# Fifteen rows of unread matmuls behind the last operations of a hybrid decoder step

## The chip, the cores and the metric

The kernel runs on one core of a Trainium2 chip. The metric is the device time of one execution in microseconds. A core has five engines that run their own instruction lists and wait for each other by semaphores: TensorE (PE; its weight loads are shown apart as PEld), VectorE (DVE), ScalarE (ACT), GpSimd (POOL) and SyncE (SP), which here issues most of the transfers.

## The reference

One inference step of one decoder layer, for a prompt of 256 tokens and 8 samples of one token, at a width of 2048. Cut to what matters:

```python
h = rmsnorm(x, g_pre_mix) * (1 + sc1) + sh1
z = h @ w_in                                  # split into the inputs of three branches
y_a = spatial_gating(u, layernorm(v))         # branch A
y_b = hgrn2(q, k, v)                          # branch B, with a state
y_c = gla(q, k, v)                            # branch C, with a state
merged = sum(sigmoid(z_gate[n]) * (y[n] @ w_branch[n]) for n in range(3))
x = x + gt1 * rmsnorm(merged @ w_out, g_post_mix)
h2 = rmsnorm(x, g_pre_mlp) * (1 + sc2) + sh2
y2 = square(relu(h2 @ w_mlp_up)) @ w_mlp_down
x = x + gt2 * rmsnorm(y2, g_post_mlp)
```

It returns x of the prompt and of the samples, the states of the branches, and the rows of v of the samples. All is in float32. Nothing of this is touched by the change.

## The kernel before, in words

The 256 prompt tokens and the 8 sample tokens are moved through TensorE together: 264 moving columns against weight tiles of 128 x 128. A float32 product is made from three products of a shorter float32 type, fp32r: each operand is split into a high and a low part (`split`, line 115: ScalarE writes the high part by a copy, VectorE the low part by a subtraction), and TensorE adds high x high, high x low and low x high in one accumulator. `granule` (lines 681 to 683) does this for nearly all of the work, 4600 times each line. Weights come from HBM in pieces of 512 KB, a few pieces ahead of use, and are split into tiles `whi` and `wlo` of [128, 2, 256]; a weight operand of a matmul is 128 columns of such a tile, in order.

The moving operands do not lie in token order. `by_two` and `apart` store the even tokens of a row in its first half and the odd ones in its second, and `moving` reads them back in turn:

```python
def moving(v):
    return v.rearrange("p (r c) -> p c r", r=2)
```

For 264 columns this takes element 0, 132, 1, 133 and so on: two runs of 132 elements, read by turns. This is called the two-way pattern here.

The stages follow one another: modulation and the input projection, the three branches with background work woven in, branch projections with gates, the output projection, the first norm, the MLP's up and down projections in blocks, and the last norm. From line 1730 on, the order of all five engines is that of the code (`manual_schedule` with all engines). This last part is what the change stands behind:

- `last_tile` (line 1744) makes the last two accumulators of the down projection; its lines 1750 to 1752 are 24 matmuls into one accumulator, 264 columns against 128 weight columns each. Line 1755 squares the result on ScalarE, line 1756 scales it on VectorE.
- `row_sums` (lines 1761 and 1762) adds up squares over the partitions with matmuls of one and of eight moving columns; line 1766 transposes.
- `rstd_sqrt` (lines 235 to 240) makes the factors `r3` of the norm.
- `by_vector` (line 1792) makes a piece of the prompt's output by one VectorE operation (line 1794) and has SP store it; this is done five times. `by_products` (line 1797) makes three pieces by two matmuls each (lines 1781 and 1798) and a ScalarE copy (line 1799), whose stores ScalarE issues (line 1790).
- POOL finishes the samples' rows (lines 1802 to 1805), TensorE transposes them (line 1809), ScalarE copies and stores them (lines 1811 and 1812).

In the trace, line 1861 is the end of the program: SP waits for the stores, and all engines meet in a barrier. Lines 1107, 1115 and 718 are operations of the branches that the prediction uses as prices: an f32 matmul, a VectorE operation with one tensor operand, and f32 matmuls with 32 weight columns.

The pools that the added code draws from: `blk()` gives tiles of 28 shared buffers, `splp` has the weight parts, `new_acc()` one of two accumulators in PSUM.

Of the kernel before, what the change touches and what calls it, by code (L numbers as in the profile page):

```python
# [8 lines left out]
F32R = mybir.dt.float32r  # L9
# [6 lines left out]
P = 128  # L16
# [14 lines left out]
CW = 256  # L31
# [33 lines left out]
def hybrid_step_kernel(  # L65
# [9 lines left out]
    V, S, T = nc.vector, nc.scalar, nc.tensor  # L75
# [4 lines left out]
    splp = ctx.enter_context(tc.tile_pool(name="splp", bufs=SPLIT_BUFS))  # L80
# [8 lines left out]
    def nm(s):  # L89
        uid[0] += 1  # L90
        return f"{s}_{uid[0]}"

    def blk(shape=None, dt=F32):
        shape = shape or [P, 4, NT]
        return blkp.tile(shape, dt, tag="b", name=nm("b"))
# [303 lines left out]
    class Queue:  # L399
# [7 lines left out]
        def step(self):  # L407
            self.held = None
            try:
                c = next(self.g[0])  # L410
                if c is READY:
                    t = now[0]
                    self.held = lambda: now[0] > t
                elif callable(c):
                    self.held = c
                else:
                    self.owed -= 1.0 if c is None else c
            except StopIteration:
                self.g.pop(0)
# [59 lines left out]
    step = [0]  # L479
# [117 lines left out]
    class Stream:  # L597
# [66 lines left out]
        def next(self):  # L664
            self.ahead()
            self.at += 1
            return self.items[self.at - 1], self.parts.pop(self.at - 1)
# [84 lines left out]
    def new_acc():  # L752
        return pmm.tile([P, 2, 512], F32, tag="mm", name=nm("mm"))
# [711 lines left out]
    x1 = [[blk([P, 1024]) for _ in range(2)] for _ in range(2)]  # L1465
# [70 lines left out]
    for m in range(8):  # L1536
        if m in PRE_AT:
            n = N_PRE // len(PRE_AT)
# [196 lines left out]
    def piece(rows, t, hf, c0):  # L1735
        return rows[t][hf][:, c0:c0 + 512]
# [52 lines left out]
    def put(eng, t, hf, c0):  # L1789
        eng.dma_start(y_prompt[0, t * P:(t + 1) * P, hf * 1024 + c0:hf * 1024 + c0 + 512], piece(yt, t, hf, c0))  # L1790

    def by_vector(t, hf, c0):
        y = piece(yt, t, hf, c0)
        V.scalar_tensor_tensor(y, y, r3[:, t:t + 1], piece(x1, t, hf, c0), ALU.mult, ALU.add)
        put(nc.sync, t, hf, c0)
# [18 lines left out]
    by_products(by_pe[2])  # L1814
    for p in ((0, 0, 512), (0, 1, 512), (1, 0, 512), (1, 1, 512)):
        by_vector(*p)
    order.__exit__(None, None, None)


# [45 lines left out]
```

## Time and profile before

| what | value |
|---|---|
| median of 2 runs | 1798.93 us (1798.78 to 1799.08) |
| the profiled execution | 1801.41 us |
| its span, first to last instruction | 1799.6 us |
| TensorE busy, matmuls | 1774.1 us, 16970 matmuls |
| TensorE, weight loads | 1686.9 us, 16970 loads |
| VectorE, ScalarE, POOL busy | 1183.5, 1002.0, 139.5 us |
| granted TensorE clock | 1.00 |
| transferred | 442.05 MB |

The profile's busy time of matmuls counts overlapped ones once; the mean of one matmul in a group (some 276 ns at lines 681 to 683) runs from its start to its modelled end, and the next one starts long before that. The spacing of matmuls is read from starts in the timeline. An f32 matmul stands as two matmul records with a load each, a transpose or an fp32r matmul as one. In a row of a group, the first number after the bar is the busy time in us and the second the mean of one in ns; in a row of a source line, the three numbers behind the count are the shortest, the median and the longest in ns. In a row of the windows, the columns are the stretch, its length, the busy time of PE, PEld, DVE, ACT and POOL with their numbers of instructions, the granted clock, the share of the DMA engines and GB/s.

### The profile page before, as it was taken

To read this page: it belongs to the slowest core of one execution; us is meant where nothing else is said; L and a number is where in the kernel's file an instruction comes from. 1 tells how busy PE (TensorE), PEld (TensorE's weight loads), DVE (VectorE), ACT (ScalarE), POOL (GpSimd) and SP (SyncE) were. 2 spreads that over 40 slices of the span, in tenths; PEclk is the share of its full clock that TensorE was granted. 3 is DMA by queue.
4 is the path that set the end of the run, shared out by engine and by line. 5 is a ranking of instruction groups with operands and counts; after the bars stand their busy time and mean duration, and the time that the engine had idled before them with its cause. 6 is when DMAs were issued, how large, how long until landed. Compare 5 with 4: busy or idle time off the path is not lost.

```text
span 1799.6 us, 42111 instructions
## 1 busy us (share of the span) xinstructions
PE 1774.1 (99%) x16970; PEld 1686.9 (94%) x16970; DVE 1183.5 (66%) x2079; ACT 1002.0 (56%) x1824; POOL 139.5 (8%) x226
## 2 busy tenths in 40 slices
PE   7999999999999999999999999999999999999998
PEld 5899999999999989999999989999999999999997
DVE  5666668696687795566555666545666666666666
ACT  5444554666856765654445656555454545454554
POOL 4232000111111112210000010000000000000000
PEclk9999999999999999999999999999999999999999
DMA  9998487788789788987877946776666666666663
GB/s 350 388 359 313 159 314 232 230 288 286 234 269 296 229 264 291 320 298 264 281 267 253 329 130 212 245 246 212 198 195 194 198 193 196 199 194 194 199 191 116
DMA packets 330179, 442.05 MB, mean 246 GB/s; under 512 B 14946, under 2 KB 276944, under 8 KB 329984
## 3 DMA queue, kind: packets, MB, share of 16 engines
q1 hardware_dynamic: 311872, 380.52, 64.0%
q0 software_dynamic: 17184, 57.85, 9.3%
q8 instruction: 133, 2.18, 0.5%
q10 hardware_dynamic: 928, 0.99, 0.2%
q14 instruction: 62, 0.51, 0.1%
HBM read 427.60 MB, written 11.70 MB: 244 GB/s over the span
## 4 chain that ended last, share of the span: by engine, by line
PE 93%; DVE 2%; DMA 2%; ACT 1%; issue 1%; SPq 0%; ACTq 0%; DVEq 0%
PE mm L681 28%; PE mm L682 28%; PE mm L683 28%; PE ada L383 3%; PE ada L315 1%; DMA raw<-in_w_in_dram 1%; DVE wlo L638 1%; PE sm L718 1%; PE sm L909 1%; PE sm L725 1%; DMA b<-in_x_prompt_dram 0%; ACT whi L634 0%; DVE b L113 0%; PE sm L1634 0%; DMA araw<-in_w_ada_dram 0%
## 5 line engine op out<-in xcount | busy, mean ns | idle before, releaser
L681 PE MATMUL mm<-b,whi 128*128 128x264 f32 x4600 | 1282.4, 279 | 1.6 <-ACT b L871 0.4
L683 PE MATMUL mm<-b,wlo 128*128 128x264 f32 x4600 | 1269.7, 276 | 1.5 <-issue 0.9
L682 PE MATMUL mm<-b,whi 128*128 128x264 f32 x4600 | 1269.6, 276 | 0.0
L638 DVE TENSOR_TENSOR wlo<-raw,whi 128x512 fp32r<-128x512 f32 x1118 | 759.8, 690 | 462.5 <-ACT whi L634 458.1
L634 ACT CAST whi<-raw 128x512 fp32r<-128x512 f32 x1118 | 682.8, 617 | 636.5 <-DVE wlo L638 319.8
L681 PEld LDWEIGHTS mm<-b,whi 128*128 128x128 f32 x4600 | 869.3, 189 | 42.1 <-issue 26.1
L682 PEld LDWEIGHTS mm<-b,whi 128*128 128x128 f32 x4600 | 869.6, 189 | 0.7 <-issue 0.5
L683 PEld LDWEIGHTS mm<-b,wlo 128*128 128x128 f32 x4600 | 869.4, 189 | 0.8 <-DVE wlo L638 0.8
L110 DVE TENSOR_TENSOR b<-b,mm 128x528 f32<-128x528 f32 (+1 forms) x137 | 95.7, 699 | 63.7 <-PE mm L683 55.8
L1802 POOL TENSOR_TENSOR gs<-b,G 128x16 f32<-128x16 f32 x1 | 0.2, 222 | 714.1 <-DVE b L110 714.1
L502 POOL DMA_DIRECT2D b<-in_w_ada_dram x64 | 46.3, 726 | 39.8 <-PE ada L315 31.1
L383 PE MATMUL ada<-araw,cT 128*32 128x512 f32 x296 | 40.9, 601 | 0.2 <-DMA araw<-in_w_ada_dram 0.2
L1166 POOL DMA_DIRECT2D out_dram<-st x32 | 23.5, 735 | 223.0 <-DVE st L1165 220.5
L634 ACT CAST whi<-araw 128x512 fp32r<-128x512 f32 x38 | 23.2, 618 | 25.1 <-PE mm L682 21.7
L315 PE MATMUL ada<-b,cT 128*32 128x256 f32 (+1 forms) x640 | 35.4, 362 | 1.4 <-DMA b<-in_w_ada_dram 1.2
L1165 DVE SCALAR_TENSOR_TENSOR st<-vbc,b,st 128x128 f32<-128x128 f32 (+1 forms) x96 | 32.4, 390 | 4.8 <-DMA out_dram<-st 2.1
L1163 ACT ACTIVATE st<-st,fs 128x128 f32<-128x128 f32 (+1 forms) x96 | 35.0, 429 | 0.0
L107 DVE TENSOR_TENSOR b<-b,b 128x512 f32<-128x512 f32 (+1 forms) x47 | 34.0, 747 | 1.6 <-ACT b L1277 0.8
L315 PEld LDWEIGHTS ada<-b,cT 128*32 128x32 f32 x640 | 18.6, 116 | 13.2 <-DMA b<-in_w_ada_dram 4.1
L383 PE MATMUL ada<-b,cT 128*32 128x512 f32 x216 | 26.2, 593 | 0.0
L638 DVE TENSOR_TENSOR wlo<-araw,whi 128x512 fp32r<-128x512 f32 x38 | 24.6, 685 | 1.5 <-ACT whi L634 1.5
L113 DVE TENSOR_TENSOR b<-gt,b 128x528 fp32r<-128x528 f32 x32 | 22.7, 710 | 3.6 <-ACT whi L634 0.5
(366 smaller groups left out, 927.8 us busy)
## 6 DMA issues: line engine op xcount, KB each, us to landing
raw<-in_w_in_dram SPq DMA_DIRECT2D x225, 512.0 KB, 4.9
raw<-in_w_mlp_down_dram SPq DMA_DIRECT2D x128, 512.0 KB, 3.5
raw<-in_w_mlp_up_dram SPq DMA_DIRECT2D x125, 512.0 KB, 3.7
araw<-in_w_ada_dram SPq DMA_DIRECT2D x74, 512.0 KB, 5.6
b<-in_w_ada_dram SPq DMA_DIRECT2D x54, 512.0 KB, 6.4
b<-in_w_ada_dram POOLq DMA_DIRECT2D x48, 512.0 KB, 10.3
raw<-in_w_branch_dram SPq DMA_DIRECT2D x48, 512.0 KB, 5.3
raw<-in_w_out_dram SPq DMA_DIRECT2D x32, 512.0 KB, 4.7
```

The lines of the kernel that those rows point to most:

```text
L107: V.tensor_tensor(o, a, b, op=ALU.mult)
L110: V.tensor_tensor(o, a, b, op=ALU.add)
L315: T.matmul(acc[32 * j:32 * j + 32, 0:n], cT[:, k, :], w[:, n * j:n * j + n], start=k == 0, stop=k == KT - 1)
L383: T.matmul(self.acc[32 * j:32 * j + 32, :], cT[:, k, :], ws[j // 2][:, j % 2 * 512:j % 2 * 512 + 512], start=k == 0, stop=k == KT - 1)
L502: queue.dma_start(w[:, i], w1[k * P:(k + 1) * P, :, self.k0 * P:(self.k0 + self.n) * P])
L634: self.last = [S.copy(hi, raw).ins, None]
L638: self.last[1] = V.tensor_tensor(lo, raw, hi.bitcast(F32), op=ALU.subtract).ins
L681: T.matmul(o, a, xh(k + j), start=first and j == 0, stop=False)
L682: T.matmul(o, a, xl(k + j), start=False, stop=False)
L683: T.matmul(o, b, xh(k + j), start=False, stop=last and j == n - 1)
L1163: S.activation(st[:, i, :], st[:, i, :], AF.Copy, scale=fs[:, h0 + i, b:b + 1])
L1165: V.scalar_tensor_tensor(st[:, i, :], v[:, i, :], k[:, h0 + i, NP + b:NP + b + 1], st[:, i, :], ALU.mult, ALU.add)
```

## The change

Behind the last `by_vector`, inside the same ordered part, it fills two tiles `xr` of [128, 1024] and two weight tiles `wr` of [128, 2, 256], all of type fp32r, with casts of the data at hand on VectorE; takes one accumulator; and issues 15 rows of 24 matmuls into it. Nobody reads the accumulator.

```diff
+    xr = [blk([P, 1024], F32R) for _ in range(2)]
+    wr = [splp.tile([P, 2, CW], F32R, tag=t, name=nm(t)) for t in ("whi", "wlo")]
+    for d in xr:
+        V.tensor_copy(d, x1[0][0])
+    for j in range(2):
+        V.tensor_copy(wr[j].rearrange("p a c -> p (a c)"), x1[1][j][:, 0:512])
+    pa = new_acc()
+
+    def seq(t, j, m=P):
+        return t[:, j // 2, j % 2 * P:j % 2 * P + m]
+
+    def step(r):
+        return lambda t, j: t.rearrange("p a c -> p (a c)").rearrange("p (c r) -> p r c", r=r)[:, j % r, 0:P]
+
+    def two(t, n=264, r=2):
+        return t[:, 0:n].rearrange("p (r c) -> p c r", r=r)
+
+    def row(w=seq, x=two, n=264, m=P, wj=None):
+        for i in range(24):
+            j = i // 3 % 4 if wj is None else wj
+            t = wr[(i % 3) // 2 if wj is None else 0]
+            T.matmul(pa[0:m, 0, 0:n], w(t, j), x(xr[i % 3 % 2]), start=i == 0, stop=i == 23)
+
+    row()
+    for n in (256, 240, 192, 128):
+        row(x=lambda t, n=n: two(t, n), n=n)
+    row(w=lambda t, j: seq(t, j, 96), m=96)
+    row(w=step(2))
+    row(w=step(4))
+    row(wj=0)
+    row(w=lambda t, j: seq(t, j, 96), m=96, x=lambda t: two(t, 128), n=128)
+    row(w=step(2), x=lambda t: two(t, 128), n=128)
+    row(w=step(4), x=lambda t: two(t, 128), n=128)
+    row(x=lambda t: two(t, 264, 4))
+    row(x=lambda t: two(t, 264, 8))
+    row(w=lambda t, j: seq(t, j, 96), m=96, x=lambda t: two(t, 264, 4))
```

Row by row: the first is as in `last_tile`; the next four have 256, 240, 192 and 128 moving columns; then 264 columns against 96 weight columns, against 128 weight columns taken at a step of 2 elements, at a step of 4, and against one and the same weight tile throughout; then 128 moving columns against 96 weight columns, at a step of 2 and at a step of 4; then 264 columns in the four-way and in the eight-way pattern (4 runs of 66, 8 runs of 33 elements, read by turns), and the four-way pattern against 96 weight columns. Where the weights are not one and the same, they go through four tiles of 128 columns, three matmuls each.

On VectorE the end of the program reads as follows; `b_24464` and `b_24465` are the tiles `xr`, `b_13646` a piece of x1, and what is in brackets is what a row waits for:

```order
 L1794 SCALAR_TENSOR_TENSOR b_23762<-b_23762,nr_24414,b_13648 128x512
 L1794 SCALAR_TENSOR_TENSOR b_23763<-b_23763,nr_24414,b_13649 128x512 [waits Activation_49]
-L1861 UNCONDITIONAL_BRANCH
+L1821 CAST b_24464<-b_13646 128x1024 [waits Pool_49]
+L1821 CAST b_24465<-b_13646 128x1024
+L1823 CAST whi_24466<-b_13648 128x512
+L1823 CAST wlo_24467<-b_13649 128x512
+L1898 UNCONDITIONAL_BRANCH
```

The four casts stand behind the last operation of `by_vector`, and the first of them waits for POOL.

On TensorE the added rows start behind the last products of `by_products`:

```order
 L1798 MATMUL mm_24427<-b_23763,vt_24431 128x512 [waits Activation_49]
 L1798 MATMUL sm_24429<-b_23762,vt_24431 128x512
-L1861 UNCONDITIONAL_BRANCH
+L1839 MATMUL mm_24472<-b_24464,whi_24466 128x264 [waits DVE_49,Activation_49]
+L1839 MATMUL mm_24472<-b_24465,whi_24466 128x264
+L1839 MATMUL mm_24472<-b_24464,wlo_24467 128x264 [waits DVE_49]
```

The first one waits for VectorE's casts and for ScalarE, which read the accumulator's buffer before; the third waits for the cast of the second weight tile. Nothing else differs in the order of any engine but the line number of the program's end.

## The prediction

> **What bounds the kernel now.** I read the page first: the span, the busy row, the chain.
>
> ```profile
> span 1799.6 us, 42111 instructions
> PE 1774.1 (99%) x16970; PEld 1686.9 (94%) x16970; DVE 1183.5 (66%) x2079; ACT 1002.0 (56%) x1824; POOL 139.5 (8%) x226
> ...
> PE 93%; DVE 2%; DMA 2%; ACT 1%; issue 1%; SPq 0%; ACTq 0%; DVEq 0%
> ```
>
> TensorE carries 93% of the chain, so a matmul added to the stream costs its full spacing. But the change adds nothing in the stream: it stands behind the last operations. So what counts is the end of the program, and I read the timeline there, engine by engine.
>
> ```profile
> 1790.18 3.78 DVE L1794 SCALAR_TENSOR_TENSOR b<-b,nr,b 128x512 f32<-128x512 f32 x5
> ...
> 1791.31 0.79 POOL L1805 TENSOR_TENSOR sqs<-gs,xsT 128x128 f32<-128x128 f32 x1
> ...
> 1793.35 1.02 PE L1798 MATMUL sm<-b,vt 128*128 128x512 f32 x2
> ...
> 1795.37 0.59 ACT L1799 COPY b<-sm 128x512 f32<-128x512 f32 x1 [0.41 <-ACT b L1799]
> ...
> 1795.99 0.34 ACTq L1790 DMA_DIRECT2D out_dram<-b  x1
> ```
>
> VectorE is done at 1790.18 + 3.78 = 1793.96, TensorE at 1793.35 + 1.02 = 1794.37. What then ends the program is ScalarE's last copy, its store issued at 1795.99, the landing of that store, and the closing barrier. The line of the kernel's end shows that barrier:
>
> ```profile
> L1861 SPq EVENT_SEMAPHORE  x11: 17/28/28, 1794.4 to 1799.5; - x11
> ...
> L1861 SPq DRAIN  x3: 7/7/7, 1798.7 to 1799.0; - x3
> ```
>
> SP's first drain, at 1798.7, comes when the stores are home; from there to the end of the span is 0.9 us. This 0.9 remains behind whatever ends last. The 5.6 us between VectorE's end (1793.96) and the span's end are the only cover that the added work has.
>
> **The change, part by part.** It removes nothing and moves nothing. It adds four casts at VectorE's end and 360 matmuls (15 x 24) at TensorE's end, no DMA and no work of SP, ScalarE or POOL. Nobody waits for the added matmuls but the closing barrier; the stores are issued as before and come home at 1798.7, under the new work.
>
> *The casts.* The first waits for POOL, whose last operation ends at 1791.31 + 0.79 = 1792.10, before VectorE is free: no cost. No cast to fp32r runs on VectorE before, so I bound it by an operation with one tensor in and one out, and by one with two tensors in:
>
> ```profile
> L1115 DVE TENSOR_SCALAR b<-b 128x1056 f32<-128x1056 f32 x1 | 0.7, 706 | 0.0
> ...
> L113 DVE TENSOR_TENSOR b<-b 128x1024 f32<-128x1024 f32 x15 | 18.4, 1226 | 0.0
> ...
> L107 DVE TENSOR_TENSOR b<-b,b 128x512 f32<-128x512 f32 x42 | 27.9, 690 | 0.7 <-ACT b L1275 0.7
> ...
> L1756 DVE TENSOR_SCALAR gt<-b,G 128x256 f32<-128x256 f32 x2 | 0.8, 382 | 0.1
> ```
>
> A cast reads one tensor, so it is nearest to L1115: about 0.70 us for 1024 columns and, between that and the 0.38 of 256 columns, some 0.45 for 512. Two of each make 2.3 us; by the two-tensor rows it would be 2 x 1.23 + 2 x 0.69 = 3.8. I take 2.3. TensorE's first added weight load then stands at 1793.96 + 2.3 = 1796.3. The accumulator that it overwrites was read out by a ScalarE copy, the last of which starts at 1795.37 and takes 0.59 (1795.96): no later.
>
> *The first row* (264 moving columns in the two-way pattern, 128 weight columns) repeats what line 1750 to 1752 do:
>
> ```profile
> 1784.16 0.28 PE L1750 MATMUL mm<-b,whi 128*128 128x264 f32 x1
> ...
> 1784.84 0.28 PE L1750 MATMUL mm<-b,whi 128*128 128x264 f32 x1
> 1784.84 0.19 PEld L1751 LDWEIGHTS mm<-b,whi 128*128 128x128 f32 x1
> ...
> 1786.75 0.28 PE L1752 MATMUL mm<-b,wlo 128*128 128x264 f32 x1
> ```
>
> From the first to the last of 24 matmuls are 23 spacings in 2.59 us: 112.6 ns each, 2.70 us a row. The 276 ns that the group's mean shows is a duration, not a spacing, and must not be multiplied by the count. The pair at 1784.84 shows that a weight load starts with the matmul ahead of it: so the spacing is the longer of moving the columns and loading the next weights.
>
> *What loading alone takes* is seen where almost nothing is moved, 1 column against 128 weight columns:
>
> ```profile
> 1786.98 0.53 PEld L1761 LDWEIGHTS sm<-cst,a 128*128 128x128 f32 x4
> ...
> 1788.00 0.52 PEld L1761 LDWEIGHTS sm<-cst,vt 128*128 128x128 f32 x4 [0.28 <-ACT vt L1755]
> ```
>
> ```profile
> L1761 PEld LDWEIGHTS sm<-cst,vt x4: 186/190/192, 1788.0 to 1788.3; 128*128 128x128 f32 x4
> ...
> L681 PEld LDWEIGHTS mm<-b,whi x4600: 186/189/192, 30.5 to 1780.2; 128*128 128x128 f32 x192
> ...
> L718 PEld LDWEIGHTS sm<-b x960: 106/109/113, 377.7 to 670.5; 128*32 128x32 f32 x192
> ```
>
> Four loads take 0.53 and 0.52 us, one 0.19: the three spacings are (0.525 - 0.19)/3 = 0.11, about 111 ns. These are f32 loads, but the fp32r loads of line 681 have the same record (189 against 190). 32 columns have 109, so a column costs (189 - 109)/96 = 0.83 ns, and 96 columns some 111 - 27 = 84 ns.
>
> So by columns: 256 moved columns would take 256/264 x 112.6 = 109.2 ns, already under the load. My rows are: eight with 264 columns (the first, 96 weight columns, both steps, one weight, and the three in four- and eight-way patterns) at 2.70, 21.6 us; six with 128 weight columns and 256 columns or fewer at 24 x 0.111 = 2.66, 16.0 us; the one with 96 and 128 at 24 x 0.084 = 2.0 us. Together 39.6 us. I charge nothing for a step or a pattern in this sum: what speaks for that stands with the rivals.
>
> *The sum.* Behind a wait, a matmul starts 0.24 us after its load:
>
> ```profile
> 1792.14 0.14 PEld L1809 LDWEIGHTS sm<-cst,sqs 128*128 128x128 f32 x1 [0.43 <-POOL sqs L1805]
> ...
> 1792.38 0.27 PE L1809 MATMUL sm<-cst,sqs 128*128 128x128 f32 x1
> ```
>
> Loads begin at 1796.3, so the first matmul starts at 1796.5; the last of 360 starts 39.5 later, at 1836.0, and its 0.28 end it at 1836.3; the barrier adds 0.9: 1837.2, against a span of 1799.6, +37.6 us. The profiled execution took 1801.41 in all, 1.8 around its span and 0.14% above the median; the difference is carried to the median: 1798.93 + 37.6 = 1836.5, +2.1%. Counted from VectorE's end, 2.3 + 0.2 + 39.5 + 0.3 + 0.9 = 43.2 us follow, of which 5.6 lie under the old end.
>
> *The clock.* TensorE idles from 1794.4 to 1796.5, 2.1 us.
>
> ```profile
> 1795.00:1798.40 3.40, 0.00 (x0) 0.00 (x0) 0.00 (x0) 0.59 (x1) 0.00 (x0) 1.00 0.86 318
> 1798.40:1799.60 1.20, 0.00 (x0) 0.00 (x0) 0.00 (x0) 0.00 (x0) 0.00 (x0) 0.52 0.00 0
> ```
>
> The granted clock (third from the right) is still 1.00 up to 1798.4, four idle microseconds on, and 0.52 after it. The added rows start before that, so I charge nothing; at half the clock for one such stretch of 3.4 us, 1.7 us would be lost.
>
> **The rivals.**
>
> ```profile
> L1798 PE MATMUL sm<-b,vt 128*128 128x512 f32 x2 | 1.0, 593 | 0.0
> ```
>
> *Steps and patterns cost.* In the two-way pattern each access of a moving operand falls 132 elements from the one before, and 264 such columns go at 112.6/264 = 0.43 ns each. If that is free only because two runs of memory can be read in turn, then four and eight runs would not be, nor weights that take one element in four. At half speed two rows (step 4) go from 2.7 to 24 x 0.218 = 5.2 us, and three (four-way, eight-way, four-way with 96) from 2.7 to 5.4: +13.1 us, 1849.6 us. For it: no four-way pattern and no stepped weight is in the trace. Against it: the two-way row is already the cheapest per column there, 0.43 ns against 0.84 for f32 columns in order (L1798 above: 1.02 for two matmuls less some 0.59 of one is 0.43 us for 512), though the types differ. [...]
>
> *Stepped weights alone are slow*, at both steps: a load of 0.83 ns a column has no slack under a spacing of 112.6, so half speed shows at once. Four rows at 5.2: +10.2 us, 1846.7. For it: every weight in the trace lies in order. Against it: the moving side jumps each 0.43 ns, twice as often as a load would have to.
>
> *Not slower by 2%: loading is no floor.* If fp32r weights hide wholly behind the matmul ahead, the seven narrow rows go by their columns: 24 x 109.2, 102.4 and 81.9 ns are 2.62, 2.46 and 1.97 us, and four rows of 128 columns (54.6 ns) 1.31 each. With the eight wide rows that is 21.6 + 7.05 + 5.24 = 33.9 us, 5.7 less than 39.6: 1830.8, +1.8%. It decides from 1.6 us on (2% is 1834.9), 9.5 ns off each of the 168 narrow matmuls. For it: no fp32r matmul with fewer than 264 columns is in the trace. Against it: the 189 ns record, the same as for loads that do set the spacing.
>
> *The rows vanish or hide*, since nobody reads them: the built program has all 360 behind the last matmul, and the cover is 5.6 us for 43.2. No chance is given to it.
>
> **How the numbers follow.** The sum as it stands 0.57, with its own range 1834 to 1840 (casts to 3.8, clock to 1.7, loads from 109 to 112.6); steps and patterns 0.15; stepped weights alone 0.12; loading no floor 0.10; other slow patterns in between or above 0.06. A measurement can tell about 2% (36 us) of this kernel from no change. Slower by over 2%: 0.50 of the first case (the rest of it falls under 1834.9), and all of the slow ones, 0.33: 0.83. Within 2%: 0.10 and 0.07, less the 0.01 that I leave for faster: 0.16. The range goes from 1831, just over the third rival, to 1850, over the first.
>
> **What will show it.** Right: four casts of 2.3 us in all from 1794.0; a first added matmul near 1796.5; eight rows of 2.7 us, the same for steps, patterns and the single weight; a flat 2.66 for 256, 240, 192 and 128 columns; 2.0 for 96 with 128; the last matmul near 1836.0. Wrong: rows that fall with the columns below 256, stepped loads with a longer record than 189 ns, spacings that differ among the two-, four- and eight-way rows, or a clock below 1.00 in the first stretch.

## The result and the profile after

The changed kernel takes 1849.41 us (1849.04 to 1849.78), 50.5 us more than before: a ratio of 1.0277, 95% interval 1.0261 to 1.0294. The prediction had 1836.5, with a range from 1831 to 1850. The time lies in the range, at its upper end, and 12.9 us above the value forecast.

The page of the kernel after, the span and the busy row:

```profile
span 1847.9 us, 42837 instructions
...
PE 1825.3 (99%) x17330; PEld 1738.4 (94%) x17330; DVE 1184.9 (64%) x2083; ACT 1001.9 (54%) x1824; POOL 139.5 (8%) x226
```

360 matmuls and 360 loads more, four VectorE instructions more, nothing else. The timeline where the added work begins:

```profile
1789.19 3.78 DVE L1794 SCALAR_TENSOR_TENSOR b<-b,nr,b 128x512 f32<-128x512 f32 x5
...
1792.89 1.28 DVE L1821 CAST b<-b 128x1024 fp32r<-128x1024 f32 x2
...
1794.09 0.41 DVE L1823 CAST whi<-b 128x512 fp32r<-128x512 f32 x1
...
1794.43 0.42 DVE L1823 CAST wlo<-b 128x512 fp32r<-128x512 f32 x1
1794.62 0.19 PEld L1839 LDWEIGHTS mm<-b,whi 128*128 128x128 f32 x1 [2.07 <-ACT b L1799]
1794.65 0.35 PE L1839 MATMUL mm<-b,whi 128*128 128x264 f32 x1 [1.27 <-DVE whi L1823]
```

VectorE is done with the output at 1792.97, 1.0 us earlier than in the execution profiled before, and the casts take until 1794.85. The first matmul doesn't wait for the last of them: it needs three of the four, which are done at 1794.09 + 0.41 = 1794.50. From there on the 15 rows follow. In the table of stretches, one row of the program is one line: the stretch, its length, then the busy times, and third from the right the granted clock. A length through 24 is the spacing.

```profile
1794.65:1797.48 2.83, 2.83 (x25) 2.83 (x25) 0.20 (x1) 0.31 (x1) 0.00 (x0) 1.00 0.79 290
1797.48:1800.15 2.67, 2.67 (x26) 2.67 (x25) 0.00 (x0) 0.00 (x0) 0.00 (x0) 1.00 0.03 6
1800.15:1802.83 2.68, 2.68 (x27) 2.68 (x25) 0.00 (x0) 0.00 (x0) 0.00 (x0) 1.00 0.00 0
1802.83:1805.49 2.66, 2.66 (x27) 2.66 (x25) 0.00 (x0) 0.00 (x0) 0.00 (x0) 1.00 0.00 0
1805.49:1808.14 2.65, 2.65 (x26) 2.65 (x25) 0.00 (x0) 0.00 (x0) 0.00 (x0) 1.00 0.00 0
1808.14:1810.87 2.73, 2.73 (x26) 2.73 (x26) 0.00 (x0) 0.00 (x0) 0.00 (x0) 1.00 0.00 0
1810.87:1813.70 2.83, 2.83 (x27) 2.83 (x25) 0.00 (x0) 0.00 (x0) 0.00 (x0) 1.00 0.00 0
1813.70:1819.30 5.60, 5.60 (x27) 5.60 (x26) 0.00 (x0) 0.00 (x0) 0.00 (x0) 1.00 0.01 3
1819.30:1821.99 2.69, 2.69 (x25) 2.69 (x25) 0.00 (x0) 0.00 (x0) 0.00 (x0) 1.00 0.00 0
1821.99:1824.01 2.02, 2.02 (x27) 2.02 (x25) 0.00 (x0) 0.00 (x0) 0.00 (x0) 1.00 0.00 0
1824.01:1826.83 2.82, 2.82 (x26) 2.82 (x26) 0.00 (x0) 0.00 (x0) 0.00 (x0) 1.00 0.00 0
1826.83:1832.44 5.61, 5.61 (x26) 5.61 (x26) 0.00 (x0) 0.00 (x0) 0.00 (x0) 0.87 0.00 0
1832.44:1837.84 5.40, 5.40 (x26) 5.40 (x26) 0.00 (x0) 0.00 (x0) 0.00 (x0) 0.50 0.02 3
1837.84:1843.37 5.53, 5.53 (x25) 4.91 (x25) 0.00 (x0) 0.00 (x0) 0.00 (x0) 1.00 0.00 0
1843.37:1846.78 3.41, 3.41 (x25) 3.31 (x23) 0.00 (x0) 0.00 (x0) 0.00 (x0) 1.00 0.00 0
```

Row by row, against the sum of the prediction:

| row | forecast, us | measured, us | more |
|---|---|---|---|
| 264 two-way, first | 2.70 | 2.83 | 0.13 |
| 256, 240, 192, 128 columns | 2.66 each | 2.67, 2.68, 2.66, 2.65 | 0.02 |
| 96 weight columns | 2.70 | 2.73 | 0.03 |
| weights at step 2 | 2.70 | 2.83 | 0.13 |
| weights at step 4 | 2.70 | 5.60 | 2.90 |
| one weight tile | 2.70 | 2.69 | -0.01 |
| 128 columns, 96 weight columns | 2.02 | 2.02 | 0.00 |
| 128 columns, step 2 | 2.66 | 2.82 | 0.16 |
| 128 columns, step 4 | 2.66 | 5.61 | 2.95 |
| four-way | 2.70 | 5.40, at half the clock | 2.70 |
| eight-way | 2.70 | 5.53 | 2.83 |
| four-way, 96 weight columns | 2.70 | 3.41 | 0.71 |

Together 52.1 us instead of 39.6: five rows hold 12.1 of the 12.5 us that are too many. What this table alone can't tell is why the same four-way pattern takes 5.40 in one row and 3.41 in another: the weight columns differ (128 and 96), and so does the clock (0.50 and 1.00).

### The profile page after: what moved, and what is told of

The parts are those of the page before. It is cut to its first block, busy times and chain, and to the rows that moved or that the text cites. A ratio compares the mean times of both kernels' runs of the same rounds, so it can differ in the third digit from the quotient of the medians.

```text
span 1847.9 us, 42837 instructions
## 1 busy us (share of the span) xinstructions
PE 1825.3 (99%) x17330; PEld 1738.4 (94%) x17330; DVE 1184.9 (64%) x2083; ACT 1001.9 (54%) x1824; POOL 139.5 (8%) x226
## 4 chain that ended last, share of the span: by engine, by line
PE 95%; DVE 2%; DMA 2%; ACT 1%; issue 1%; SPq 0%; DVEq 0%; ACTq 0%
PE mm L681 28%; PE mm L682 27%; PE mm L683 27%; PE ada L383 3%; PE mm L1839 3%; PE ada L315 1%; PE sm L718 1%; DMA b<-in_w_ada_dram 1%; PE sm L909 1%; PE sm L725 1%; DVE wlo L638 1%; DMA b<-in_x_prompt_dram 0%; DMA araw<-in_w_ada_dram 0%; PE sm L1634 0%; PE sm L1265 0%
## 5 line engine op out<-in xcount | busy, mean ns | idle before, releaser
L1839 PE MATMUL mm<-b,whi 128*128 128x264 f32 (+6 forms) x248 | 50.6, 312 | 1.3 <-DVE whi L1823 1.3
L1839 PEld LDWEIGHTS mm<-b,whi 128*128 128x128 f32 (+1 forms) x248 | 43.2, 215 | 2.5 <-ACT b L1799 2.1
L1839 PE MATMUL mm<-b,wlo 128*128 128x264 f32 (+6 forms) x112 | 35.3, 315 | 0.0
```

The costliest lines, as they stand in the source:

```text
L1839: T.matmul(pa[0:m, 0, 0:n], w(t, j), x(xr[i % 3 % 2]), start=i == 0, stop=i == 23)
```

## The experiments

All of them are the changed kernel with other rows in the place of the 15. The spacings named are lengths of stretches through 24; where the first matmuls of a row are out of step with the rest (they wait, or follow a row of another kind), the spacing of the others is named.

**The same rows in another order.** Patterns ahead, step 4 last:

```diff
     row()
+    row(x=lambda t: two(t, 264, 4))
+    row(x=lambda t: two(t, 264, 8))
+    row(w=lambda t, j: seq(t, j, 96), m=96, x=lambda t: two(t, 264, 4))
...
+    row(w=step(4))
+    row(w=step(4), x=lambda t: two(t, 128), n=128)
```

> The same 15 rows in another order: the four-way, eight-way and four-way-with-96 rows stand second to fourth, the two step-4 rows last. In the changed kernel the granted clock was 0.5 from 1831.0 to 1837.8, over the end of the narrow step-4 row and the whole four-way row. Theory A: the narrow step-4 row leaves the array idle so long that the clock halves, and the four-way row's 220 ns is 264 columns at half the clock; at full clock it is at 140 to 160 ns (the row with 96 weight columns had 142). Then the four-way row takes 3.4 to 3.8 us instead of 5.4, the clock halves only behind or in the last row, and the span is 1.5 to 2 us shorter than the changed kernel's. Rival B: the pattern costs 220 ns at any clock; then the row stays at 5.3 us and the span is within 0.5 us of the changed kernel's.

The second to fourth rows and the last:

```profile
1796.63:1800.04 3.41, 3.41 (x27) 3.41 (x25) 0.00 (x0) 0.00 (x0) 0.00 (x0) 1.00 0.02 5
1800.04:1805.57 5.53, 5.53 (x26) 4.90 (x25) 0.00 (x0) 0.00 (x0) 0.00 (x0) 1.00 0.00 0
1805.57:1809.00 3.43, 3.43 (x26) 3.43 (x24) 0.00 (x0) 0.00 (x0) 0.00 (x0) 1.00 0.00 0
...
1838.41:1843.86 5.45, 5.45 (x25) 5.45 (x24) 0.00 (x0) 0.00 (x0) 0.00 (x0) 0.80 0.00 0
```

At a granted clock of 1.00 the four-way row takes 3.41 us, 142 ns a matmul, with 128 weight columns, and 3.43 with 96. The clock now falls in the last row, the narrow one with step 4 (0.80 over the row), and nothing stands behind it that could suffer. The span is 1845.2 instead of 1847.9: 2.7 us less, of which the four-way row gives 2.0; the added work also began 0.8 us earlier in this execution. Theory A holds, rival B falls.

**Fifteen plain rows.**

```diff
+    for _ in range(15):
+        row()
```

> All 15 rows are the first one (264 columns two-way, 128 weight columns in order). Theory: what the prediction put behind VectorE's end (casts, first wait, barrier) and its row price of 2.70 us were right, and the whole miss lies in steps and patterns. Then the 15 rows take 40.6 us, and the kernel 1837.5 us within 1.5. Rival: part of the miss is a fixed cost (a slow start, a clock drop, a longer end) that plain rows pay too; then over 1840.

1837.92 us (1836.22 to 1838.44) against 1799.87 of the kernel before on the same chip, a ratio of 1.0209 (1.0192 to 1.0226): 38.05 us more. The prediction's terms give 38.5 for this kernel (its 37.6 with 15 x 2.70 = 40.5 in the place of 39.6). So casts, waits, barrier and cover together were priced to within half a microsecond, and nearly the whole miss lies in the steps, the patterns and the clock.

**Without the narrow step-4 row.** Only that row is taken out of the changed kernel:

```diff
-    row(w=step(4), x=lambda t: two(t, 128), n=128)
```

> The changed kernel without its twelfth row (128 columns, step 4). That row itself took 5.6 us. Theory A (it also halves the clock under the row behind it): the four-way row falls from 5.4 to 3.4 us, so the kernel is 7.6 us shorter, 1841.8 us, and the clock is 1.00 to the end. Rival: the clock halves for another reason, or not at all; then only the row's own 5.6 us go, 1843.8 us.

1842.28 us (1841.52 to 1842.55), against 1799.67 before on the same chip: 42.6 us more, a ratio of 1.0236 (1.0219 to 1.0253), where the change has 50.5. The span falls from 1847.9 to 1840.3, by 7.6, though the row itself was worth 5.6. The other 2.0 come from the four-way row, which now stands right behind the narrow step-2 row:

```profile
1826.79:1830.25 3.46, 3.46 (x26) 3.46 (x26) 0.00 (x0) 0.00 (x0) 0.00 (x0) 1.00 0.00 0
```

This settles the clock: 2.0 of the 12.5 us fall on one row, at 0.50 behind the narrow step-4 row and at 1.00 without it.

**What makes the clock fall.**

```diff
...
+    base(4)
+    for _ in range(4):
+        row(w=step(4), x=lambda t: two(t, 128), n=128)
+    base(8)
+    for _ in range(4):
+        row(w=step(4))
+    base(8)
+    for _ in range(8):
+        row(x=lambda t: two(t, 128), n=128)
+    base(8)
+    for _ in range(8):
+        row(x=lambda t: two(t, 64), n=64)
+    base(8)
+    for _ in range(4):
+        row(w=step(4), x=lambda t: two(t, 192), n=192)
+    base(8)
```

> Long stretches of one kind, eight plain rows between them: 4 rows of 128 columns with step-4 weights (the array moves columns for 54.6 of 233 ns, 23%), 4 rows of 264 with step 4 (47%), 8 rows of 128 with weights in order (48% of 112), 8 rows of 64 in order (24%), 4 rows of 192 with step 4 (34%). Theory K, the clock halves when the array moves columns for too small a share of a stretch of some 3.4 us: halved in the first and the fourth stretch, not in the second and third; the fifth tells where between 24 and 47% the limit is. Rival L, weight loads count as use: then the fourth stretch, in which loads follow each other without a gap, stays at full clock. While the clock is halved the plain rows behind a stretch have 220 to 225 ns, and it comes back some 3.4 to 7 us later.

```profile
1805.03:1808.44 3.41, 3.41 (x16) 3.41 (x16) 0.00 (x0) 0.00 (x0) 0.00 (x0) 1.00 0.00 0
1808.44:1828.92 20.48, 20.48 (x90) 20.48 (x90) 0.00 (x0) 0.00 (x0) 0.00 (x0) 0.50 0.00 1
1849.37:1871.77 22.40, 22.40 (x98) 22.40 (x97) 0.00 (x0) 0.00 (x0) 0.00 (x0) 1.00 0.00 1
1893.37:1914.75 21.38, 21.38 (x194) 21.38 (x193) 0.00 (x0) 0.00 (x0) 0.00 (x0) 1.00 0.01 2
...
1941.57:1975.70 34.13, 34.13 (x161) 34.13 (x161) 0.00 (x0) 0.00 (x0) 0.00 (x0) 0.50 0.00 0
...
1999.59:2020.07 20.48, 20.48 (x90) 20.48 (x90) 0.00 (x0) 0.00 (x0) 0.00 (x0) 0.50 0.00 0
```

Here `base(k)` stands for k plain rows. The five lines behind the first are the five kinds in turn (the halved ones from the moment of the fall to the return). Array use is the share of the spacing in which columns move, at 112.5/264 = 0.426 ns each; by this the five kinds have 23, 48, 49, 24 and 35%, a point more in three cases than was expected. The clock halves, to 0.50, at 23%, 24% and 35% of array use and stays at 1.00 at 48% and 49%. In the first kind it falls 4.24 us behind the start of the step-4 rows (1804.20): the first line, 3.41 us from 1805.03 to 1808.44 that are all in these rows, still has 1.00. In the changed kernel the stretch at 0.50, from 1831.01 to 1837.84, was 6.83 us, twice 3.41. The halved stretches here last 20.48, 34.13 and 20.48 us, 6, 10 and 6 times 3.41, and the times between them, 112.65 and 23.89 us, are 33 and 7 times it. The full clock came back 2.4, 3.2 and 1.9 us behind the ends of the three stretches (1826.55, 1972.52, 2018.15), sooner than the 3.4 to 7 us expected. Rival L falls: in the fourth kind one load follows another without a gap (loads are busy for all the 34.13 us of its line), and the clock halves all the same. The busy columns say nothing of this; PE reads as fully busy in every one of these lines.

By an estimate from these rows, what counts is the columns moved in 3.41 us, not the time that they take. At half the clock 264 columns take 220 ns (the four-way row of the changed kernel, behind its first matmuls), and so a column 0.83; the 192-column rows then move columns for 160 of 233 ns, 69%, and yet the clock stays halved until the plain rows. In columns, the three kinds that halve it move at most 2810 in 3.41 us (192 each 233 ns); the two that don't halve it move at least 3860 (264 each 233 ns). A row of a later run, 512 columns each 490 ns, kept 1.00 with some 3570, so the estimate puts the limit of this case between that and 2810; no run tests it apart.

**Weights at steps, and loads alone.**

```diff
...
+    for r in (3, 4):
+        row(w=wide(r))
+        row()
+    for r in (6, 8):
+        row(w=far(r))
+        row()
+    for m in (128, 96, 64, 32):
+        row(w=lambda t, j, m=m: seq(t, j, m), m=m, x=lambda t: two(t, 64), n=64)
+        row()
...
```

> Rows with 264 two-way columns and weights at steps of 2, 3, 4, 6 and 8 elements, a plain row between any two. Theory E, a load pays for each group of 4 elements (16 bytes) that it opens: step 2 at 118 ns as in the changed kernel, step 3 between 118 and 233, step 4 at 233, and 6 and 8 at 233 as well, since from 4 on each element opens one group. Rival F, the load pays by the distance: step 6 near 350 and step 8 near 465 ns. Then rows of 64 columns with 128, 96, 64 and 32 weight columns: the load alone, 112, 85, 58 and 31 ns if it goes by its columns. Then step 4 with 64 and 32 weight columns against 264 columns: 117 and 112.5 ns if step 4 costs 1.82 ns a column.

`wide` takes 128 elements of a weight tile at the step named; `far` takes them from the tiles `xr`, since steps 6 and 8 reach past the 512 elements of a weight tile. Steps 2, 3, 4, 6 and 8, then step 4 with 64 weight columns:

```profile
1796.58:1799.41 2.83, 2.83 (x26) 2.83 (x25) 0.00 (x0) 0.00 (x0) 0.00 (x0) 1.00 0.02 6
...
1802.11:1806.32 4.21, 4.21 (x27) 4.21 (x26) 0.00 (x0) 0.00 (x0) 0.00 (x0) 1.00 0.00 0
...
1809.02:1814.62 5.60, 5.60 (x27) 5.60 (x26) 0.00 (x0) 0.00 (x0) 0.00 (x0) 1.00 0.00 0
...
1817.32:1822.69 5.37, 5.37 (x26) 5.37 (x25) 0.00 (x0) 0.00 (x0) 0.00 (x0) 1.00 0.02 3
...
1825.39:1831.12 5.73, 5.73 (x26) 5.73 (x25) 0.00 (x0) 0.00 (x0) 0.00 (x0) 1.00 0.00 0
...
1851.66:1854.53 2.87, 2.87 (x26) 2.87 (x25) 0.00 (x0) 0.00 (x0) 0.00 (x0) 1.00 0.00 0
```

118, 175, 233, 224 and 239 ns. Beyond step 4 the distance makes little difference: theory E holds, rival F falls (350 and 465 ns expected at steps 6 and 8). 128 weights at steps 2, 3 and 4 open 64, 96 and 128 groups of four elements; 118, 175 and 233 through these is 1.84, 1.82 and 1.82 ns a group, and 64 weights at step 4 have 120/64 = 1.87 (117 ns was expected); 32 weights at step 4 stay at 112.5, as expected (an estimate: three rows of 2.70 us, this one and a plain one on each side of it, fill the time from 1854.53 to the end of the matmuls, some 1.2 us ahead of the span's end at 1863.8). In order there are 32 groups (58 ns by that price), and the 0.83 ns an element is longer: loads alone, against 64 moved columns, stand at 112, 85, 58 and 32 ns for 128, 96, 64 and 32 columns. For weights, then, two elements of each group cost 6 ns more than four (118 against 112), and one element of each doubles the load (233).

**Moving patterns.** A plain row behind each:

```diff
...
+    for r, s in ((1, 264), (2, 132), (4, 66), (6, 44), (8, 33), (12, 22), (2, 133), (2, 512), (4, 68), (4, 72), (4, 256), (8, 36), (8, 128)):
+        row(x=lambda t, r=r, s=s: runs(t, r, s))
+        row()
+    for q in (2, 3):
+        row(x=lambda t, q=q: t[:, 0:264 * q].rearrange("p (c q) -> p q c", q=q)[:, 0, :])
+        row()
```

> Each row of 24 has 264 moving columns in another pattern, always against 128 weight columns in order, with a plain two-way row behind each so that the clock stays up: 1 run in order, 2 runs of 132, 4 of 66, 6 of 44, 8 of 33, 12 of 22, then 2 runs 133 or 512 apart, 4 runs 68, 72 or 256 apart, 8 runs 36 or 128 apart, then every second and every third element. Theory C, the number of runs decides: one and two runs at 112.5 ns, four at 140 to 160, six between, eight and twelve at 230 or more, whatever the distance between runs. Rival D, the distance of the runs decides (66 and 33 elements don't fill whole groups of 4 elements, 132 does): then 4 runs 68 or 72 apart go at 112.5 ns like 2 runs 132 apart, and 2 runs 133 apart are slow. Every second element: 112.5 by a theory in which two elements of a group of 4 are enough, over 200 if each jump costs; every third between 112.5 and 230.

One, two, four, six and eight runs, and every second element:

```profile
1793.84:1796.88 3.04, 3.04 (x25) 3.04 (x26) 0.19 (x1) 0.31 (x1) 0.00 (x0) 1.00 0.72 268
...
1799.57:1802.27 2.70, 2.70 (x26) 2.70 (x25) 0.00 (x0) 0.00 (x0) 0.00 (x0) 1.00 0.00 0
1804.97:1808.38 3.41, 3.41 (x26) 3.41 (x25) 0.00 (x0) 0.00 (x0) 0.00 (x0) 1.00 0.00 0
1811.08:1814.75 3.67, 3.67 (x26) 3.67 (x25) 0.00 (x0) 0.00 (x0) 0.00 (x0) 1.00 0.00 0
1817.46:1822.98 5.52, 5.52 (x26) 4.93 (x25) 0.00 (x0) 0.00 (x0) 0.00 (x0) 1.00 0.00 0
...
1880.54:1886.19 5.65, 5.65 (x27) 4.98 (x25) 0.00 (x0) 0.00 (x0) 0.00 (x0) 1.00 0.00 0
```

Two to eight runs have 112, 142, 153 and 230 ns; twelve have 242. The distance between runs matters little: 112.5 at 132, 133 and 512 elements apart, 142 at 66, 68 and 72 (146 at 256), 230 at 33 and 36. Only eight runs 128 apart stand out, at 257, and no run shows why. So far theory C, and rival D falls. But three rows contradict C. In order, one run, the row is slower than two runs: its first matmuls wait for the casts, but its last 18, from 1794.68 to 1796.88, still have 122 ns. And every second element, also one run, has 235, and every third as well, where 112.5 to 230 was expected of it.

**Patterns against weight columns.**

```diff
+    for r in (2, 4, 8):
+        for m in (128, 96, 64, 32):
+            row(w=lambda t, j, m=m: seq(t, j, m), m=m, x=lambda t, r=r: two(t, 264, r))
...
```

> Two-way, four-way and eight-way rows of 264 columns, each against 128, 96, 64 and 32 weight columns in order; then four- and eight-way with 128 and with 512 columns. Theory I, reading the moving operand is the limit: spacing does not change with the weight columns, 112.5, 142 and 230 ns, and follows the moved columns: 512 four-way 275, 512 eight-way 446; with 128 columns both are at the load's 112. Rival J, moving reads and weight loads get in each other's way: the four- and eight-way spacings fall as the weight columns do, by 20 ns or more from 128 to 32.

Eight-way with 32 weight columns, then with 512 moving columns:

```profile
1834.15:1839.69 5.54, 5.54 (x25) 3.12 (x24) 0.00 (x0) 0.00 (x0) 0.00 (x0) 1.00 0.00 0
...
1854.55:1866.31 11.76, 11.76 (x25) 5.03 (x24) 0.00 (x0) 0.00 (x0) 0.00 (x0) 1.00 0.00 0
```

Four-way stays at 142 ns and eight-way between 229 and 231, whether 128 or 32 columns are loaded; with 128 moving columns the two rows together take 5.39 us, 112 ns a matmul, like the load. So in these rows reading the moving operand is the limit and loads don't enter: theory I, and rival J falls. 512 columns take 282 and 490, where 275 and 446 were expected: four-way follows the columns within 3%, eight-way is 10% above.

**Several elements of a run at a turn.** 256 columns against 32 weight columns, so that the 109 ns of the columns (256 x 0.426), and not the load's 32, are the floor:

```diff
...
+    for r in (2, 4, 8):
+        go(lambda t, r=r: two(t, 256, r))
+        for q in (2, 4):
+            go(pairs(r, q))
...
```

> Moving operands of 256 columns against 32 weight columns, so that the load (32 ns) is out of the way and the array itself needs 109 ns. Rows: in order; then for 2, 4 and 8 runs by turns: one element of each run at a turn, two at a turn, four at a turn (with the runs starting at whole groups of 4 elements); then every second and every fourth element, each in one run and in two runs by turns. Theory M, what costs is the change to another group of 4 elements when more than two are in use: eight runs at 223 ns with one element a turn fall to about 120 with four at a turn (64 changes instead of 256) and lie between with two. Rival N, the number of runs decides: eight runs stay near 223 and four near 138 however many elements a turn takes. In order near 118. Every second element in one run near 229 (264 had 236); in two runs by turns it falls towards 118 if two runs by turns always overlap, and stays near 229 if it is the distance between elements that counts. Every fourth in one run at 229 to 235 under both.

Four runs with four elements at a turn, then eight runs with one, two and four:

```profile
1827.97:1831.23 3.26, 3.26 (x26) 2.74 (x24) 0.00 (x0) 0.00 (x0) 0.00 (x0) 1.00 0.00 0
1833.93:1839.20 5.27, 5.27 (x26) 3.10 (x24) 0.00 (x0) 0.00 (x0) 0.00 (x0) 1.00 0.00 0
1841.93:1847.31 5.38, 5.38 (x26) 3.10 (x24) 0.00 (x0) 0.00 (x0) 0.00 (x0) 1.00 0.00 0
1850.05:1852.87 2.82, 2.82 (x27) 2.59 (x24) 0.00 (x0) 0.00 (x0) 0.00 (x0) 1.00 0.02 6
```

Eight runs: 220, 224 and 117 ns with one, two and four elements at a turn. Four runs: 139, 228 and 136. Two: 109, 166 and 123. Every second element: 227 in one run, 116 in two by turns; every fourth 231 in both. The number of runs doesn't decide (rival N: eight runs with four at a turn have 117), but theory M fails too: two elements at a turn should lie between one and four and are the slowest of the three.

**Two streams.** One reading fits most of these rows: even and odd columns are read as two streams, and each of them pays for its groups of four elements as a load does (1.82 ns each; a hit is one element read from a group). This run tests it, for the most part on patterns that had not been tried:

```diff
...
+    go(lambda t: t[:, 0:256])
+    go(lambda t: t[:, 0:256].rearrange("p (c r q) -> p c q r", r=2, q=4))
+    go(lambda t: t[:, 0:256].rearrange("p (c r q) -> p c q r", r=2, q=2))
+    go(lambda t: t[:, 0:768].rearrange("p (c q) -> p q c", q=3)[:, 0, :])
+    go(lambda t: t[:, 0:768].rearrange("p (r c q) -> p q c r", r=2, q=3)[:, 0])
...
```

> 256 moving columns against 32 weight columns, plain rows between. Theory O, made from the rows so far: the columns are read as two streams, the even and the odd ones, and each stream pays some 1.8 ns for each group of 4 elements that it opens, as the weight load does, unless its 0.83 ns an element is longer. In order: 2 hits a group, 64 groups a stream, 115 to 118 ns. By turns from two neighbouring groups of 4 (0, 4, 1, 5, 2, 6, 3, 7, then on): each stream takes a whole group, 109 ns, the array's own time, although it is one run of memory. By turns from halves of one group (0, 2, 1, 3): 2 hits a group a stream, 115 to 118 like in order. Every third element in one run: a new group each time, near 228; in two runs by turns: 96 groups a stream, near 171. Every second in two runs 116 and the two-way pattern 109, as before. Rival P, it is the number of runs, or the distance from one column to the next, that decides: then the neighbouring groups are no better than in order (115 to 118), and every third element in two runs stays at 228 or falls to 109.

In this order:

```profile
1795.95:1798.73 2.78, 2.78 (x26) 2.59 (x25) 0.00 (x0) 0.00 (x0) 0.00 (x0) 1.00 0.02 6
1801.43:1804.05 2.62, 2.62 (x26) 2.61 (x25) 0.00 (x0) 0.00 (x0) 0.00 (x0) 1.00 0.00 0
1806.76:1809.53 2.77, 2.77 (x26) 2.59 (x24) 0.00 (x0) 0.00 (x0) 0.00 (x0) 1.00 0.00 0
1812.23:1817.66 5.43, 5.43 (x26) 3.12 (x25) 0.00 (x0) 0.00 (x0) 0.00 (x0) 1.00 0.01 3
1820.38:1824.51 4.13, 4.13 (x27) 2.88 (x25) 0.00 (x0) 0.00 (x0) 0.00 (x0) 1.00 0.00 0
```

116, 109, 115, 226 and 172 ns, where 115 to 118, 109, 115 to 118, 228 and 171 were expected; every second element in two runs has 116 again, the two-way pattern 109. Rival P falls on the second row (one run of memory, a short jump, and yet the floor, 109) and on the fifth (172).

## Why the prediction was right or wrong

- *The end of the program, the casts, the barrier:* right. The first matmul stood 1.68 us behind VectorE's end, 2.54 forecast. The four casts took 1.96 of the 2.3, the first matmul needed three of them (done 1.53 behind VectorE's end), and it came 0.03 and not 0.24 behind its load. From the last matmul's start (1846.66) to the span's end were 1.3 us, 1.2 forecast. Fifteen plain rows confirm the sum within half a microsecond.
- *The load as the floor of narrow rows:* right. 256, 240, 192 and 128 columns are flat at 2.65 to 2.68 us, and 128 columns against 96 weight columns have 2.02, as summed. The rival in which loads are no floor is refuted.
- *"I charge nothing for a step or a pattern in this sum":* this is the step that failed. It left out 5.85 us for the two step-4 rows, 0.3 for the step-2 rows, 2.8 for the eight-way row, and 0.7 for each four-way row. The reason given was that the two-way pattern jumps at every column and is free, so that jumps are free. By the two-stream reading, which the five spacings of the last run bear out, this was no evidence: a stream sees every other column only, and in the two-way pattern (109 ns for 256 columns) each stream walks one run in order, four elements to a group. So by this reading the pattern that seems to jump at every column makes no stream jump at all.
- *"The added rows start before that, so I charge nothing" for the clock:* right for the gap ahead of the rows, which the argument was about, and wrong in looking nowhere else. The clock fell to 0.50 inside the added rows, in the narrow step-4 row, which moves columns for 54.6 of its 233 ns; without that row it stayed at 1.00. It cost 2.0 us.
- *The rival "Steps and patterns cost"* came to 1849.6 us, and 1849.41 was measured. It had step 4 right in kind (5.2 forecast, 5.6 measured) and the eight-way row (5.4 and 5.5). But it had both four-way rows at 5.4, where one takes 3.41 and the other reached 5.40 only at half the clock. So the agreement to 0.2 us is partly luck. Its mechanism, two runs that may be read in turn, is not what the runs show: two neighbouring groups of one run, read by turns, are as fast (109 ns for 256 columns). That the time lies in the range at all is owed to this rival, which set the upper end and was given a chance of 0.15; the sum itself had 37.6 us for what came to 50.5.
- *From span to median:* the span was to grow by 37.6 and grew by 48.3: 12.5 more in the rows, 0.9 less ahead of them, and 1.0 less because the execution profiled after reached the end of its old work 1.0 us sooner. The profiled execution before was 2.5 us above its median and the one after 0.4; that makes the other 2.1 of the 12.9.

## What to carry to other kernels

Price an operand's pattern by the groups of four elements that each reader of it opens, not by how far one access lies from the next (weights at steps 4, 6 and 8 take 233, 224 and 239 ns); a pattern that is in the trace and costs nothing says little of another one. Lay fp32r weights in order (112 ns a load, against 118 at step 2 and 233 at step 4), and moving columns so that the even and the odd ones each run through whole groups of four elements: two halves by turns do it, and so do neighbouring groups of four (109 ns each for 256 columns, against 116 in order). And when a stretch makes TensorE wait for loads, look at the granted clock behind it: with columns moving for 23, 24 and 35% of the time it fell to 0.50, 4.2 us into the first of these stretches, and a row behind such a stretch paid for it (the four-way row, 5.40 us at 0.50 and 3.41 at 1.00).

## What the runs showed of the hardware

- Reading moving fp32r columns in order costs 122 ns for 264 columns where the two-way pattern costs 112.5, 8% more. By these two spacings the kernel's layout of tokens is worth some 8% on the matmuls of its three main lines, each 28% of the chain before; this is an estimate, as no run changes the layout.
- A step-4 load takes 233 ns at a granted clock of 1.00 and of 0.50 (the second narrow step-4 row of the run on the clock, all of it at 0.50, has 5.60 us as well), while rows that go by their loads in order, 64 columns against 128 weight columns, went from 112 to 213 (5.12 us a row). So in these rows the price of a group doesn't go by the granted clock. The two rows at half clock:

```profile
1809.75:1815.35 5.60, 5.60 (x26) 5.60 (x26) 0.00 (x0) 0.00 (x0) 0.00 (x0) 0.50 0.00 0
...
1941.80:1946.92 5.12, 5.12 (x25) 5.12 (x26) 0.00 (x0) 0.00 (x0) 0.00 (x0) 0.50 0.00 0
```

- What stays open is what a stream pays for groups that it comes back to. In the four-way pattern, by the two-stream reading, each stream goes to and fro between two groups and needs 139 ns for 256 columns, less than the 228 of a new group each time and more than 109; with two elements at a turn from two runs 166, with six runs 153 for 264 columns. The two-stream reading says nothing of these rows. Some others it misses: with four elements at a turn each stream reads two elements of a group, which should give 115 to 118 ns as in order, and eight runs do (117), but two runs take 123 and four runs 136; and eight runs 128 elements apart take 257 where 132 groups at 1.82 would be 240. The remaining rows lie within 6% of it, but a reading that fits is not the circuit.
